# Weaving the latent projections of an attention layer into the last Strassen product of the layer before it

## The chip, the cores and the metric

The kernel runs on one NeuronCore of a Trainium2 chip. The metric is the device time of one execution in microseconds (us). TensorE (PE) multiplies, VectorE (DVE) and ScalarE (ACT) do the elementwise work, GpSimd (POOL) and SyncE (SP) mostly issue DMAs. "Before" took 1385.39 us, the median of three runs (1384.32 to 1385.72).

## The reference

A backbone of two layers over 256 latent tokens and 256 context tokens, model width 1024, all in float32. Layer 0 mixes tokens with a bidirectional chunkwise mLSTM, layer 1 with multi-head latent attention; behind each mixer stands a gated convolutional FFN of inner width 2816, and behind every sub-layer a gated residual with LayerNorm. The place of this change is the seam between the FFN of layer 0 and the attention of layer 1:

```python
x  = layer_norm(ALPHA * x + gate * ffn(h))            # end of layer 0, both streams
h  = x * (1 + scale) + shift                          # input of the attention
def _mla_kv(h, w_dkv, kv_norm, w_ukv, ang):
    ckv, k_rope = split(h @ w_dkv, [256])             # 256 + 64 columns
    if ang is not None: k_rope = axial_rope(k_rope, *ang)
    kv = rms_norm(ckv, kv_norm) @ w_ukv               # 8 heads x (128 key + 128 value)
def _mla_q(h, w_dq, q_norm, w_uq, ang):
    q = rms_norm(h @ w_dq, q_norm) @ w_uq             # 384 columns; 8 heads x (128 + 64)
y = attend(q_latent, [k_context; k_latent], [v_context; v_latent]) @ w_out
```

The latent stream alone is put out, so in layer 1 the context gives keys and values only, and no queries. Its norm, its projection `dkv` and what follows are still needed before the first scores.

## The kernel before, in words

**Products in three matmuls.** Every float32 operand is held as a high and a low part in the type fp32r. `mm3` (lines 398 to 401) issues three matmuls for each product: high by high, high by low, low by high. The halves come from `split` (line 403): ACT casts the high part (line 404), DVE subtracts it to get the low one (line 405).

**Weights as a stream.** `Stream` holds all weight chunks (128 x 1024 floats, 512 KB) in one written-out order, made by `_plan`. SP's queue loads a chunk into a raw buffer (line 293); `_split` casts it on ACT (line 335) and subtracts on DVE (line 338) into a `w` tile (three of them) or, for chunks called wide, into two tiles of the class `u`. There are 31 `u` tiles for nearly everything that is large, and 15 half-size ones (`s2`). `use` hands the next chunk to a product and splits up to eight chunks ahead, as far as tiles and a limit (`st.limit`) allow; `pump` moves the limit and splits up to it.

**Who orders the work.** The program text gives each instruction its priority; a scheduler orders each engine's queue at compile time with an estimate of the times, and each engine then runs its queue in that order. Inside `manual_schedule` for PE, PE's own order is the program's. Background work (`bg`) is written as generators, of which `tick` runs the next steps, `drain` all of them; that too only sets the place in the program.

**The last product of layer 0** (`w_fout0`, line 1368 on) multiplies the FFN's activations by its output weights, both halves of the tokens and of the columns, in Strassen-like products. The first four products (yt2, y11, yt3, yt1) run chunk by chunk in turn, six chunks each, 24 steps. Then come y21, yt4 and y22 in the order `YLAST`: y21 chunks 0 and 1, yt4 0 to 5, y21 2 to 5, y22 0 to 5. A chunk is twelve matmuls of 512 columns (line 1403), the last one six. The activations of these three products were written to DRAM before and are read again by `operand`: one read of up to 256 KB on ACT's queue (line 1384), a copy on ACT (line 1390) and a subtraction on DVE (line 1391) three calls later. There are 18 such reads; in the first four products `operand` is called at every second step from step 11 on, seven times, then once a chunk.

**The seam.** The residual add (`add`, lines 1461 and 1462) and the norm by sums (`z_norm`: squares on ACT, line 1511, roots, line 1515, scaling on ACT, line 1518) make `z`, two row tiles for the latent tokens and two for the context. `ln_T` transposes `z` on PE (line 1214, four transposes into one PSUM tile), applies scale and shift (lines 1221 to 1223) and splits into `hl` (latent) or `hc` (context) (lines 1226, 1227). In the old order the generator `latent` gets its first tick behind y21 chunk 2, does the norm of both tiles in one step and puts its four groups of transposes behind y22 chunks 0, 1, 2 and 3. All of y22 is done before `mla_down` begins:

- `dkv` of the latent tokens (48 matmuls of 320 columns), then the whole `context` generator (residual add and norm of the context tiles), then the latent rows (`dkv_rows`: RMS norm by lines 1525 to 1528, rotary key, copies, line 1563);
- `dq` (48 matmuls of 384 columns), `pump`, the transposes `ckT` of the latent rows (line 1575), the RMS norm of the queries `cq`;
- `ctx_T`, the 16 transposes of the context's `z`; `ukn(1)`, the latent keys (48 matmuls of 256 columns); `uv((2, 3))`, the latent values; `dkv` of the context with its rows.

`mla` goes on with the transposes `cqT` (line 1672), the rotary queries `qr` (18 matmuls), `ckT` of the context, rope on `qr` (lines 1536 to 1538, 1699, 1700), `queries(0)` and `(1)`, `ukn(0)`, `uv((0, 1))`, `rotary(0)` and the loop over heads. The residual for the attention's output (`ln_x`, lines 1242 and 1243, with loads and writes on POOL's queue) runs from `bg` in between. PE's written order covers `YLAST` and `mla_down`, not the first four products and not `mla`.

**The end of attention.** The output product `aout` is followed by `ln_rows` (lines 1156 to 1188), `ln_T` and the first chunks of the second FFN (`fin1`). Between the steps of that norm `st.pump(fi + QB)` and `st.pump(fi + QC)` allow fin1's chunks 2 and 3, then 4 and 5, to be split.

Of the kernel before, what the change touches and what calls it, by code (L numbers as in the profile page):

```python
# [57 lines left out]
         [("y21", j) for j in range(YTURN, 6)] + [("y22", j) for j in range(6)])  # L58
# [13 lines left out]
def _plan():  # L72
# [35 lines left out]
    for n, j in YLAST:  # L108
        add((n, 0, j), cols[j])
    for c, m in enumerate((3, 3, 2)):  # L110
        add(("dkv", 0, c), m * 320, True)
    for c in range(4):
        add(("dq", 0, c), 768, True)
    for c in range(2):
        add(("ukn", 0, c), 1024, True)
    for c in range(2):
        add(("uv", 0, c), 1024, True)
    for c, n in enumerate((2, 1)):
        add(("uqr", 0, c), n * 512)
    for c in range(3):  # L120
        add(("uqn", 0, c), 1024)
# [249 lines left out]
class K:  # L371
# [774 lines left out]
    def ln_rows(self, pss, xres, gate, fin=None):  # L1146
# [3 lines left out]
        for t in range(2):  # L1150
# [33 lines left out]
            if fine and t == 0:  # L1184
                nc.scalar.activation(z[:, 0:512], z[:, 0:512], AF.Identity, bias=nm, scale=rs)
            else:
                nc.vector.tensor_scalar(z[:, 0:512], z[:, 0:512], mv[:, 0:1], rs, op0=ALU.subtract, op1=ALU.mult)
            nc.scalar.activation(z[:, 512:1024], z[:, 512:1024], AF.Identity, bias=nm, scale=rs)
# [179 lines left out]
    def w_fout0(self, x1d, kv0, lat_T, down):  # L1368
# [5 lines left out]
        parts = [(names[n], i) for n, i in YLAST]  # L1374
# [41 lines left out]
        for i in range(6):  # L1416
            for name, ps, x in (("yt2", p6, "S2"), ("y11", p1, "1"), ("yt3", p7, "S3"), ("yt1", p5, "S1")):
# [7 lines left out]
                if n >= 11 and n % 2:  # L1425
                    operand()
# [39 lines left out]
        def latent():  # L1466
            yield from add(1, lo, p7)
            for _ in self.z_norm(z[2:4], sums[2:4]):
                pass
            yield  # L1470
            yield
# [6 lines left out]
        with self.tc.manual_schedule(engines={mybir.EngineType.PE}):  # L1478
            for name, i in YLAST:
                if (name, i) == ("y21", YTURN):  # L1480
                    self.drain()
                    self.bg = [latent()]
                w = st.use((name, 0, i))
                ps, more = {"y21": (p1, True), "yt4": (p7, True), "y22": (p5, True)}[name]
                prod(ps, names[name], w, i, more)
                if name == "yt4" and i in (0, 3):
                    rows(1 if i == 0 else 0)
                if (name, i) == ("yt4", 3):
                    for b in range(2):
                        nc.vector.tensor_tensor(p5[b], p5[b], t[b], op=ALU.subtract)  # L1490
                    self.bg = [add(1, hi, v)]
                if name == "y22" and i < 2:
                    next(low)
                self.tick(2 if name == "y22" and i else 1)
                operand()
                if (name, i) == ("y21", 5):
                    low = add(0, lo, p1)
            self.drain()
            self.fa = self.fd = None
            down(context(), z)  # L1500


    def z_norm(self, zs, sums):

        nc = self.nc
        for z, v in zip(zs, sums):
# [6 lines left out]
            yield  # L1513
# [3 lines left out]
            nc.vector.tensor_tensor(v[:, 0:1], v[:, 0:1], v[:, 2:3], op=ALU.mult)  # L1517
            nc.scalar.activation(z, z, AF.Identity, bias=v[:, 0:1], scale=v[:, 2:3])
            yield
# [95 lines left out]
    def mla_down(self, hl, hc, context, ctx_T):  # L1615

        nc, st = self.nc, self.st
        kv0 = [x[0] for x in st.order].index(("ukn", 0, 0))
        wd = [st.use(("dkv", 0, c), hold=True) for c in range(3)]
# [3 lines left out]
        nc.vector.memset(self.krT[64:128, 1].bitcast(F32), 0.0)  # L1623
        rows = self.dkv_mm(hl, wd)
        for _ in context:
            pass
# [356 lines left out]
```

## Time and profile before

| what | value |
|---|---|
| median of three runs | 1385.39 us |
| profiled execution | 1388.08 us, of which 1386.3 us are its span |
| granted TensorE clock, mean | 0.993 |
| PE busy | 1356.3 us (98%) |
| DVE, ACT, POOL busy | 1061.5, 705.3, 122.5 us |
| DMA moved | 291.86 MB |
| y22's first transposes to the first scores | 1034.4 to 1118.3 us |

A row of a timeline has the start, the length, the engine with its line, the operation, output and inputs, and in brackets the idle time of the engine ahead of it with what ended it. When several like instructions follow each other they make one row (x12). Matmuls overlap, so one matmul's length is longer than the distance to the next. In the list of waits stand the engine and line that waited, the one that ended the wait, the total in us, the number of waits and the longest.

### The profile page before, as it was taken

Reading aid. Unit: us, or ns where it says so; the run is one execution under the profiler, and the core shown is the slowest. Engines: PE = TensorE matmul, PEld = TensorE weight load, DVE = VectorE, ACT = ScalarE, POOL = GpSimd, SP = SyncE. Lnnn points to the kernel's source line nnn. Section 1 sums busy time; section 2 is a strip of 40 time slices with the busy share of each in tenths; the row PEclk is TensorE's granted clock in tenths of the full one; section 3 lists DMA queues with packets and bytes.
Section 4 is the critical chain, followed back from the end, with each engine's and each line's share of the span. In section 5 each row is a group of like instructions: output and inputs, shape, how many; then the busy total and the mean of one; then the engine's idle time right before and its main releaser. Section 6 shows DMA issues by size and latency. Waiting matters only on the chain.

```text
span 1386.3 us, 19100 instructions
## 1 busy us (share of the span) xinstructions
PE 1356.3 (98%) x6903; PEld 1143.7 (83%) x6903; DVE 1061.5 (77%) x1710; ACT 705.3 (51%) x1189; POOL 122.5 (9%) x215
## 2 busy tenths in 40 slices
PE   7999999999999999999999999999998999999997
PEld 3788888888788888878798888888877988999986
DVE  6599757687698697788799878668788689777773
ACT  6585534435444545374643434334578467455560
POOL 0033000011011011120002000001100100000000
PEclk9999999999999999999999999999999999999999
DMA  9689847789656364756747877735867226357750
GB/s 336 223 290 324 290 154 248 238 280 308 216 196 209 100 234 137 245 193 223 239 142 246 298 229 236 237 113 163 248 249 242 85 84 221 107 189 227 208 183 31
DMA packets 94014, 291.86 MB, mean 211 GB/s; under 512 B 11704, under 2 KB 20536, under 8 KB 93920
## 3 DMA queue, kind: packets, MB, share of 16 engines
q1 hardware_dynamic: 67808, 215.64, 47.0%
q0 software_dynamic: 17472, 57.57, 13.4%
q10 hardware_dynamic: 8640, 17.44, 3.5%
q8 instruction: 54, 0.88, 0.3%
q14 instruction: 40, 0.33, 0.1%
HBM read 260.02 MB, written 30.58 MB: 210 GB/s over the span
## 4 chain that ended last, share of the span: by engine, by line
PE 91%; ACT 3%; DVE 3%; DMA 2%; issue 1%; SPq 0%; DVEq 0%; ACTq 0%
PE fin L399 9%; PE fin L400 9%; PE fin L401 9%; PE y L1403 7%; PE tok L399 6%; PE tok L401 6%; PE tok L400 6%; PE qk L399 4%; PE qk L401 4%; PE qk L400 4%; PE y L400 3%; PE y L401 3%; PE y L399 3%; PE up L399 2%; PE up L400 2%; PE up L401 2%
## 5 line engine op out<-in xcount | busy, mean ns | idle before, releaser
L338 DVE TENSOR_TENSOR w<-raw,w 128x1024 fp32r<-128x1024 f32 x286 | 344.1, 1206 | 165.0 <-ACT w L335 164.2
L335 ACT CAST w<-raw 128x1024 fp32r<-128x1024 f32 x286 | 297.0, 1039 | 326.7 <-PE fin L401 100.8
L400 PE MATMUL fin<-h,w 128*128 128x256 f32 (+1 forms) x696 | 231.7, 333 | 0.0
L401 PE MATMUL fin<-h,w 128*128 128x256 f32 (+1 forms) x696 | 231.4, 333 | 0.0
L399 PE MATMUL fin<-h,w 128*128 128x256 f32 (+1 forms) x696 | 231.2, 333 | 0.1
L528 DVE SCALAR_TENSOR_TENSOR junk<-ar,bc 128x1024 f32<-128x1024 f32 x128 | 155.8, 1217 | 4.8 <-ACT bc L570 2.9
L401 PEld LDWEIGHTS fin<-h,w 128*128 128x128 f32 x696 | 132.2, 190 | 12.9
L399 PEld LDWEIGHTS fin<-h,w 128*128 128x128 f32 x696 | 131.9, 190 | 13.2 <-ACT h L1226 0.3
L400 PEld LDWEIGHTS fin<-h,w 128*128 128x128 f32 x696 | 132.2, 190 | 12.8 <-DVE h L1227 0.2
L399 PE MATMUL qk<-xc,w 128*128 128x512 f32 x256 | 100.7, 393 | 0.0
L401 PE MATMUL qk<-xc,w 128*128 128x512 f32 x256 | 99.9, 390 | 0.0
L400 PE MATMUL qk<-xc,w 128*128 128x512 f32 x256 | 99.8, 390 | 0.0
L399 PEld LDWEIGHTS qk<-xc,w 128*128 128x128 f32 x256 | 48.1, 188 | 10.1 <-issue 0.4
L401 PEld LDWEIGHTS qk<-xc,w 128*128 128x128 f32 x256 | 48.1, 188 | 10.0
L400 PEld LDWEIGHTS qk<-xc,w 128*128 128x128 f32 x256 | 48.1, 188 | 9.6
L399 PE MATMUL up<-hT,w 128*128 128x512 f32 x128 | 50.4, 394 | 0.5 <-ACT hT L404 0.5
L338 DVE TENSOR_TENSOR wu<-raw,wu 128x1024 fp32r<-128x1024 f32 (+3 forms) x37 | 43.0, 1177 | 10.2 <-ACT wu L335 10.0
L400 PE MATMUL up<-hT,w 128*128 128x512 f32 x128 | 50.1, 392 | 0.5 <-DVE hT L405 0.5
L401 PE MATMUL up<-hT,w 128*128 128x512 f32 x128 | 50.1, 391 | 0.3 <-DVE w L405 0.3
L399 PE MATMUL tok<-w,hT 128*128 128x512 f32 x128 | 49.8, 389 | 0.0
L400 PE MATMUL tok<-w,hT 128*128 128x512 f32 x128 | 49.8, 389 | 0.0
L401 PE MATMUL tok<-w,hT 128*128 128x512 f32 x128 | 49.8, 389 | 0.0
(436 smaller groups left out, 2970.5 us busy)
## 6 DMA issues: line engine op xcount, KB each, us to landing
raw<-in_ws SPq DMA_DIRECT2D x287, 512.0 KB, 4.5
ar<-in_adaT SPq DMA_DIRECT2D x80, 512.0 KB, 4.8
adaw<-in_ada_w SPq DMA_DIRECT2D x32, 256.0 KB, 6.7
raw<-in_ws POOLq DMA_DIRECT2D x13, 512.0 KB, 7.1
xmd<-xr POOLq DMA_DIRECT2D x16, 256.0 KB, 5.2
xcd<-cv POOLq DMA_DIRECT2D x16, 256.0 KB, 4.9
xs<-xmd POOLq DMA_DIRECT2D x16, 256.0 KB, 5.5
od<-o ACTq DMA_DIRECT2D x16, 256.0 KB, 2.4
```

Of the source, the lines that this page charges most:

```text
L335: k.nc.scalar.copy(h[:, :cols], src)
L338: k.nc.vector.tensor_sub(l[:, :cols], src, h[:, :cols])
L399: mm(out, w[0], x[0], start=start, stop=False)
L400: mm(out, w[0], x[1], start=False, stop=False)
L401: mm(out, w[1], x[0], start=False, stop=stop)
L528: nc.vector.scalar_tensor_tensor(o, w, 1.0, self.bc[j], op0=ALU.mult, op1=ALU.mult, accum_out=col[:, k, j:j + 1])
L1403: nc.tensor.matmul(ps[b], a[:, p, ts], w[q][:, cs], start=j == 0 and n == 0 and not more, stop=j == 10 and n == 2, skip_group_check=True)
```

## The change

`YLAST` takes in three more entries (dkv and dq, and the transposes ckT, between chunks of y22):

```diff
-         [("y21", j) for j in range(YTURN, 6)] + [("y22", j) for j in range(6)])
+         [("y21", j) for j in range(YTURN, 6)] + [("y22", j) for j in range(4)] +
+         [("dkv", 0), ("y22", 4), ("dq", 0), ("ckT", 0), ("y22", 5)])
```

The weight order follows it (dkv's three chunks before y22 chunk 4, dq's four before y22 chunk 5) and goes on with ukn, uqr, two chunks of uqn, uv, the last of uqn; it was ukn, uv, uqr, uqn. `mla_down` is gone: its parts are `lat_kv` (weights of dkv, latent dkv and its rows) and `lat_q` (dq and the RMS norm of its rows), called from the loop over `YLAST`, and the rest moved into `mla`. PE's written order now covers the first four products, `YLAST` and `mla` up to `rotary(0)`.

```diff
-                if n >= 11 and n % 2:
+                if n >= 5 and n % 4 != 3:
                     operand()
...
         def latent():
             yield from add(1, lo, p7)
-            for _ in self.z_norm(z[2:4], sums[2:4]):
-                pass
-            yield
-            yield
+            yield from self.z_norm(z[2:4], sums[2:4])
+            for _ in range(3):
+                yield
             yield from lat_T(z[2:4])
...
+            if name == "dkv":
+                self.drain()
+                self.lat_kv(hl)
+                continue
+            if name == "dq":
+                self.lat_q(hl)
+                st.pump(kv0 + 2)
+                continue
+            if name == "ckT":
+                self.dkv_T(self.rows, 2)
+                continue
             if (name, i) == ("y21", YTURN):
                 self.drain()
                 self.bg = [latent()]
+                self.tick(3)
...
-                self.tick(2 if name == "y22" and i else 1)
+            self.tick(4 if name == "y22" and i else 1)
```

So the latent transposes come in two groups of eight, behind y22 chunks 1 and 2. `z_norm` does its three phases (squares, roots, scaling) for both row tiles together, with a yield after each phase; it had two yields for each tile. `context` has the same body and is now stepped through inside `mla`:

```diff
+    def mla(self, hc, context, ctx_T, residual):
+        for _ in range(2):
+            next(context)
         st.limit = [x[0] for x in st.order].index(("aout", 0, 0))
+        self.wk = [st.use(("ukn", 0, c)) for c in range(2)]
...
+        next(context)
+        self.ukn(1)
+        for _ in context:
+            pass
...
         queries(0)
+        ctx_T()
         queries(1)
+        rows = self.dkv_mm(hc, self.wd)
+        st.unhold("dkv")
+        rows = self.dkv_rows(rows, 0)
+        self.wv = [st.use(("uv", 0, c)) for c in range(2)]
+        self.uv((2,))
+        qr = []
...
+        self.dkv_T(rows, 0)
+        self.uv((3,))
         self.ukn(0)
         self.uv((0, 1))
+        for _ in residual:
+            pass
         rotary(0)
```

Behind the attention the splits of fin1's chunks 2 to 5 are queued behind the last two scalings of the norm, on DVE and ACT, and stand in the program behind its transposes:

```diff
-        k.tick(1)
-        st.pump(fi + QB)
-        k.tick(1)
-        st.pump(fi + QC)
+        k.tick(2)
         k.drain()
+        with tc.issue_after(k.lv.ins), tc.issue_after(k.la.ins):
+            st.pump(fi + QC)
```

`k.lv` and `k.la` are the last DVE and ACT scalings of `ln_rows`; `issue_after` fixes only the order of issue on an engine.

159 lines of the change are left out of this document (74 added, 85 removed).

## Prediction

> **What bounds the kernel now.** I read the page first, for the engine that sets the time.
>
> ```profile
> PE 1356.3 (98%) x6903; PEld 1143.7 (83%) x6903; DVE 1061.5 (77%) x1710; ACT 705.3 (51%) x1189; POOL 122.5 (9%) x215
> ...
> PE 91%; ACT 3%; DVE 3%; DMA 2%; issue 1%; SPq 0%; DVEq 0%; ACTq 0%
> ```
>
> TensorE (PE) is busy in 98% of the span and holds 91% of the chain that ended last. The change removes no matmul, so it can only win time in which PE stood still or ran slowly. The list of what PE waited for, cut to 980 to 1200 us where the touched code runs, says how much that is:
>
> ```profile
> PE ckT L1575 <- DVE ckr L1528: 4.8, 2, 3.0
> PE zT L1214 <- ACT z L1518: 1.9, 1, 1.9
> PE zT L1214 <- DVE z L1187: 1.8, 1, 1.8
> PE qr L399 <- ACT cqT L1674: 0.6, 1, 0.6
> ```
>
> The reader sees three waits that the change moves (ckT, the first zT, qr) and one that stands behind the attention and whose work keeps its place (zT on z L1187). The timeline of PE shows what follows a wait:
>
> ```profile
> 1036.65 0.55 PE L1214 MATMUL zT<-ident,z 128*128 128x128 f32 x3 [1.94 <-ACT z L1518]
> 1036.95 4.58 PE L1403 MATMUL y<-w,fz 128*128 128x512 f32 x12
> 1041.38 0.60 PE L1214 MATMUL zT<-ident,z 128*128 128x128 f32 x4
> 1041.73 3.00 PE L1403 MATMUL y<-w,fz 128*128 128x512 f32 x12
> ...
> 1070.85 0.33 PE L1575 MATMUL ckT<-ident,ckr 128*128 128x128 f32 x1 [2.97 <-DVE ckr L1528]
> 1073.06 1.33 PE L1575 MATMUL ckT<-ident,ckr 128*128 128x128 f32 x5 [1.88 <-DVE ckr L1528]
> 1074.18 3.62 PE L1214 MATMUL zT<-ident,z 128*128 128x128 f32 x16
> 1077.45 0.56 PE L399 MATMUL kn<-ckT,wu 128*128 128x256 f32 x1
> ```
>
> ```profile
> 1034.40:1052.40 18.00, 16.06 (x72) 13.02 (x72) 15.98 (x27) 16.95 (x31) 0.00 (x0) 0.91 0.45 145
> 1067.90:1078.00 10.10, 5.27 (x24) 5.05 (x25) 8.27 (x24) 8.48 (x22) 2.16 (x4) 0.67 0.73 242
> ```
>
> After the 1.94 us wait the same twelve matmuls take 4.58 us and then 3.00 us, and the stage table (us, busy PE, PEld, DVE, ACT, POOL, granted clock, DMA share, GB/s) grants 0.91 of the clock over those 18 us: 0.09 x 18 = 1.6 us lost. In the second stage the 16 zT start from 1074.18 to 1077.45, 0.204 us apart, where eight transposes at full clock take 0.87 us, 0.109 each (row below); that is 1.5 us lost, and the five ckT lose (1074.18 - 1073.06) - 5 x 0.109 = 0.6 us, the first kn some 0.3 us.
>
> ```profile
> 1128.01 0.87 PE PT L1764 x8
> ```
>
> So what can be won at most is 1.94 + 1.6 (first zT), 2.97 + 1.88 + 2.4 (ckT and the zT behind it) and 0.6 (qr): **11.4 us**, 0.8% of the time.
>
> [...]
>
> **The change part by part.**
>
> *The latent norm and its transposes.* Three background steps run before the product y21[2], the norm of both row tiles goes in three joint phases, and the transposes come in two bursts of eight behind y22[1] and y22[2], instead of four bursts of four from y22[0] on. One product of twelve matmuls of 512 columns stands in front more. In the stage of the first four products (row below) 179 such matmuls take 40 us, 0.223 each:
>
> ```profile
> 960.00:1000.00 40.00, 40.00 (x179) 33.11 (x178) 27.84 (x29) 16.82 (x20) 6.61 (x10) 1.00 0.76 203
> ```
>
> That is 2.7 us; z came 1.94 us late, so this alone covers it. Besides, the adds that feed the norm waited behind weight splits on DVE (VectorE):
>
> ```profile
> 1021.59 0.69 DVE L1461 TENSOR_TENSOR zp<-y,gate 128x512 f32<-128x512 f32 x1
> 1022.20 1.22 DVE L338 TENSOR_TENSOR w<-raw,w 128x1024 fp32r<-128x1024 f32 x1
> ...
> 1026.62 0.68 DVE L1461 TENSOR_TENSOR zp<-y,gate 128x512 f32<-128x512 f32 x1
> ```
>
> The second add started 5 us after the first, both traced one product apart; traced together they should follow each other. The wait goes: -3.5 us. What is late next is the copying of hl: eight pairs on ACT (ScalarE) between the first burst and dkv. ACT was busy 16.95 of 18.00 us there.
>
> ```profile
> 1047.79 0.60 PE L1214 MATMUL zT<-ident,z 128*128 128x128 f32 x4
> ```
>
> ```profile
> 1050.42 0.83 ACT L335 CAST wu<-raw 128x768 fp32r<-128x768 f32 x1
> ```
>
> The dkv product now starts two products (y22[4], y22[5], 18 matmuls, 4.0 us) earlier, but the last burst ends some 6.5 us earlier too (behind y22[2] and 16 transposes, 1034.4 + 2 x 2.7 + 1.7 = 1041.5, for the 1048.4 of the row), and four of the reread activations are copied before. I take 0.2 us of waiting, from 0 to 1.0 (hl[7] caught behind casts of dq's weights, 0.83 us each as in the second row).
>
> *dkv and dq between the chunks.* In the old order the context norm stands ahead of the latent rows on ACT and DVE: PE leaves dkv at 1059.40 (first row below), and the second tile's row comes with the wait that ends at 1073.06 (above). Now y22[4] (2.7 us) and dq lie behind dkv:
>
> ```profile
> 1059.40 0.34 PE L399 MATMUL dq<-wu,hl 128*128 128x384 f32 x1
> ...
> 1067.55 0.34 PE L401 MATMUL dq<-wu,hl 128*128 128x384 f32 x1
> ```
>
> 48 matmuls in 8.3 us. The cover is 11 us. The chain it has to hide can be read off the context's own pass, which had little ahead of it (PE's last dkv, then ACT, then DVE):
>
> ```profile
> 1095.92 0.31 PE L401 MATMUL dkv<-wu,hc 128*128 128x320 f32 x1
> ```
>
> ```profile
> 1095.82 0.38 ACT L1525 ACTIVATE ckr<-dkv 128x256 f32<-128x256 f32 x1 [2.44 <-PE dkv L401]
> ...
> 1096.63 0.47 ACT L1526 ACTIVATE rs<-rs,keps 128x1 f32<-128x1 f32 x2
> ```
>
> ```profile
> 1098.31 0.48 DVE L1528 TENSOR_SCALAR ckr<-dkv,rs 128x256 f32<-128x256 f32 x1
> ...
> 1099.22 0.18 DVE L1563 COPY ckr<-ckr 128x64 f32<-128x64 f32 x1
> ```
>
> ```profile
> L1675 DVE SCALAR_TENSOR_TENSOR cqT<-cqT,sm 128x256 fp32r<-128x256 f32 x3 | 1.4, 472 | 0.0
> ```
>
> PE is past its last dkv at 1096.1 (48 matmuls in 7 us, 0.15 each), the last copy ends at 1099.4: 3.3 us, 1.4 of them the three cqT operations of the group row, which ran between. 11 us hide that with room, so the ckT waits go: -7.2 us. Without that cover it would be 1 to 2 us.
>
> *The new wait: cqT.* The queries' rows are now wanted right behind dq, with six ckT transposes (0.7 us) and y22[5] (six matmuls, 1.3 us) as cover, 2.0 us. The same chain on 384 columns, without the cqT operations, is 3.3 - 1.4 plus about 0.5 for the wider square and scaling: 2.4 us. Behind the waiting cqT stands all of PE. So at least 0.4 us; with a ckT copy and a weight split (1.2 us) caught in between up to 2.0, and 1.6 us of lost clock on top if it passes the length of the wait at the first zT. The wait of 0.6 us at qr cost no clock, 1.00 being granted in its stage, the second row:
>
> ```profile
> 1078.00:1097.00 19.00, 18.88 (x126) 17.68 (x124) 8.87 (x19) 8.11 (x21) 0.00 (x0) 1.00 0.06 19
> 1097.00:1118.00 21.00, 20.48 (x133) 18.63 (x134) 20.20 (x40) 11.38 (x21) 2.17 (x4) 1.00 0.45 151
> ```
>
> I take +1.5.
>
> *qr* now follows ukn(1), 48 matmuls, so its wait of 0.6 goes. *Context norm behind the latent keys:* its squares and scalings (rows below: on ACT four of the first kind, 0.9 with their read-out, and two of the second; on DVE four adds of 0.7) fall beside ukn(1), qr and queries(0), 84 matmuls at 0.15 (126 in 18.88 us, above), some 12 us of PE:
>
> ```profile
> 1029.38 0.71 ACT L1511 ACTIVATE jk<-z,zs 128x512 f32<-128x512 f32 x1
> ...
> 1035.36 1.24 ACT L1518 ACTIVATE z<-z,zs 128x1024 f32<-128x1024 f32 x1
> ```
>
> The chain is 4 x 0.9 + 2 x 1.2 + 4 x 0.7, some 9 us. Hidden: 0 us, and up to 3 if ACT's queue holds much else. The residual's loads and writes move on POOL's queue with it; no wait of PE in the list names POOL.
>
> *Context keys:* dkv_rows(0) is covered by uv((2,)), 12 matmuls of 512 columns, 2.7 us, against a chain of 1.9 to 3.3 us, with rope rows as possible neighbours on DVE. Bounds 0 and 1.1, I take +0.5.
>
> *DVE in front of the scores.* DVE is the fullest engine beside PE. In the attention itself:
>
> ```profile
> 1118.00:1160.00 42.00, 41.49 (x271) 37.02 (x270) 36.79 (x76) 28.64 (x63) 5.00 (x9) 1.00 0.27 96
> ```
>
> Between 1067.9 and 1118 DVE did 8.27 + 8.87 + 20.20 = 37 us (rows above); with the context's four adds and the small steps of its norm, done ahead of that so far and now behind the last product, some 41, while PE's part of that stage, without its waits and slow stretches and with y22[5] in it, is 50 - 2.97 - 1.88 - 0.6 - 2.4 + 1.3 = 43 us. Of the 41, the residual and the last v (7 us) need not precede the scores. DVE was full for 20.20 of 21.00 us before without a wait of PE. Bounds 0 and 3, I take +0.7.
>
> *Rereads in the first four products.* 14 instead of 7 of the 18 reads are issued there, from ACT's queue, with a copy on ACT and a subtraction on DVE of 512 columns each, half of a split (1.2 us for 1024 columns, above): 7 x 0.6 = 4 us more on engines that have room (27.84 of 40 us on DVE, 16.82 on ACT in the stage's row), and 4 us less where ACT was full. 0 us, and up to 1. The weights' order on SP's queue changes only within the stage; ukn is wanted at about 1066, 11 us earlier than now, and its second half was split by 1061.7:
>
> ```profile
> 1060.50 1.21 DVE L338 TENSOR_TENSOR wu<-raw,wu 128x1024 fp32r<-128x1024 f32 x1
> ```
>
> *The end of attention.* Four weight chunks of fin1 are now split behind the last norm instead of ahead of it. In the old trace the last of them starts at 1179.43, PE's last y at 1184.42:
>
> ```profile
> 1179.43 1.21 DVE L338 TENSOR_TENSOR wu<-raw,wu 128x1024 fp32r<-128x1024 f32 x1
> ```
>
> ```profile
> 1184.42 0.28 PE L401 MATMUL y<-wu,oT 128*128 128x256 f32 x1
> ```
>
> So the wait there (z L1187, above) hangs on PE itself: nothing to win. Behind the norm, four splits of 1.2 us on DVE, and about as much on ACT, lie beside the copies of h. Bounds -0.3 and +2.5, I take +0.5.
>
> **Sum:** -3.5 - 7.2 - 0.6 + 0.2 + 1.5 + 0.5 + 0.7 + 0.5 = -7.9 us. The profiled execution took 1388.08 us with a span of 1386.3; the median of the runs is 1385.39, 2.7 lower. Off the median: 1377.5 us. By the bounds alone the forecast lies between 1374 (new waits nearly nil) and 1385 (all of them at their ends).
>
> **The rivals.** *The waits move.* Two new waits (cqT and the scores, say) each pass the length that costs clock: 2 x (1.9 + 1.6) = 7.0 us back instead of 3.4. For it: the cover of cqT is shorter than its chain. Against: no other cover is. Gain some 4 us: 1382.
>
> *The chains stay as late.* ACT and DVE are ordered when the kernel is compiled, by an estimate; if splits still go ahead of the adds and rows, the waits stay though the program is rewritten. For it: the add held up by 5 us. Against: each chain has gained a cover longer than its lateness. 1385.4.
>
> [...]
>
> *Slower: a queue held by a tile slot.* In the old trace ACT stood still for 6.63 us in front of a copy of v, because its target tile (one of 31) came free only with dkv; DVE stood behind it:
>
> ```profile
> 1090.98 2.40 ACT L404 CAST v<-v 128x512 fp32r<-128x512 f32 x4 [6.63 <-PE dkv L401]
> ```
>
> It cost PE nothing, since PE had all of dkv to do. I count 30 to 34 such tiles wanted at ctx_T in the new order (kn 8, wd 6, wk 4, wv 4, z, ckT, krT, qn, hc 4). If ACT is held there again, hc comes late with only queries(1), 2.1 us, as cover, and DVE's 41 us wait behind it: at the rate of the attention stage (36.79 of 42.00, 0.88) they need 47, and with 6.6 us of standing still PE comes out of its 43 us some 10 late. With one lost stretch of clock (1.6) and the waits of the sum at cqT and fin1 (2.0) that is 14 us against the 11.4 won: 1387 to 1389. It decides from the point where the hold outlasts queries(1). [...] Against it: dkv's own first matmuls free hc and wd tiles.
>
> **How the numbers follow.** Forecast 0.60, waits move 0.18, slow clock 0.03, chains as late 0.06, slower 0.13. A measurement of this kernel tells about 0.2% (2.8 us) from no change. Faster: 0.60 + 0.18 + 0.03, less a tail of the second, 0.80; within: the unchanged case with that tail, 0.07; slower: 0.13. The range runs from 1373.5 (all 11.4 us, rounded out) to 1386.5, which leaves out the slower rival.
>
> **What would show it.** No wait of PE at zT behind y22[1]; ckT behind y22[4]/dq without wait; a granted clock of 1.00 from 1030 to 1060; a wait of 0.4 to 2 us at cqT; dkv of the context without a wait. I am wrong if hc or ckT of the context is waited for by more than 3 us, if the first fin1 matmuls stand behind splits, or if a wait appears in the first four products.

## The result: no difference that can be measured

The changed kernel takes 1385.86 us (median of 12 executions, 1384.04 to 1388.58), the kernel before, measured again beside it, 1386.46 us (12 executions): ratio 0.9995, 95% interval 0.9986 to 1.0004. The forecast of 1377.5 us was 8.4 us too low: 7.3 us because a gain of 7.9 us was forecast and 0.6 us came, and 1.1 us because the kernel before, measured again, was slower than the 1385.39 us from which the forecast started. Two executions of the kernel before in later rounds, of 1688.40 and 2751.32 us, are left out of the ratios. The profiled execution of the changed kernel took 1384.17 us, with a span of 1382.1 us.

### The profile page after: what moved, and what is told of

Read it like the earlier page. It is cut to its first block, busy times and chain, and to the rows that moved or that the text cites. A ratio compares the mean times of both kernels' runs of the same rounds, so it can differ in the third digit from the quotient of the medians.

```text
span 1382.1 us, 19113 instructions
## 1 busy us (share of the span) xinstructions
PE 1353.0 (98%) x6903; PEld 1139.1 (82%) x6903; DVE 1062.1 (77%) x1710; ACT 704.6 (51%) x1189; POOL 122.5 (9%) x215
## 4 chain that ended last, share of the span: by engine, by line
PE 90%; DVE 4%; ACT 3%; DMA 2%; issue 1%; SPq 0%; DVEq 0%; ACTq 0%
PE fin L404 9%; PE fin L405 9%; PE fin L406 9%; PE y L1409 7%; PE tok L404 6%; PE tok L406 6%; PE tok L405 6%; PE qk L404 4%; PE qk L406 4%; PE qk L405 4%; PE y L405 3%; PE y L406 3%; PE y L404 3%; PE up L404 2%; PE up L406 2%; PE up L405 2%
```

## The profile after

TensorE is the bound as before (page of the changed kernel, first part; before it was busy 1356.3 us):

```profile
PE 1353.0 (98%) x6903; PEld 1139.1 (82%) x6903; DVE 1062.1 (77%) x1710; ACT 704.6 (51%) x1189; POOL 122.5 (9%) x215
```

The list of PE's waits in the changed kernel, 980 to 1200 us, answers to the four rows shown of before (total, times, longest; the lines of the changed file are up to 20 higher):

```profile
PE zT L1220 <- DVE z L1192: 2.5, 1, 2.5
PE dkv L404 <- DVE qn L1721: 1.2, 1, 1.2
PE fin L404 <- ACT h L1232: 1.1, 1, 1.1
PE o L404 <- ACT PT L409: 1.0, 1, 1.0
PE y L1409 <- ACT w L340: 0.9, 1, 0.9
PE y L1409 <- DVE w L343: 0.7, 2, 0.5
PE cqT L1682 <- DVE cq L1547: 0.5, 1, 0.5
PE ckT L1594 <- DVE ckr L1547: 0.4, 1, 0.4
PE zT L1220 <- ACT z L1537: 0.3, 1, 0.3
PE fin L405 <- DVE h L1233: 0.3, 1, 0.3
PE ckT L1594 <- DVE ckr L1582: 0.3, 1, 0.3
PE kn L405 <- DVE ckT L1599: 0.2, 1, 0.2
```

The waits aimed at are gone: the first zT, qr, and of 4.8 us at ckT 0.7 are left. In their place stand nine smaller ones, and the wait behind the attention has grown. The gaps of at least 0.15 us between PE's matmuls from 1000 us on add up to 9.9 us before and 9.4 us after. **Nearly all of the idle time has only moved.**

Where it moved shows in the three stretches from the first row of y on `fs` to the first scores, on to the first `fin1`, and on to the first row of fout1 (us; busy PE, PEld, DVE, ACT, POOL; granted clock, DMA share, GB/s). First the kernel before, then the changed one:

```profile
941.72:1118.31 176.59, 169.17 (x859) 146.20 (x858) 142.44 (x238) 106.40 (x181) 13.14 (x21) 0.97 0.62 199
1118.31:1190.08 71.77, 69.14 (x427) 61.08 (x426) 61.60 (x116) 46.55 (x88) 5.53 (x10) 0.98 0.42 147
1190.08:1317.17 127.09, 127.09 (x1059) 127.09 (x1057) 91.08 (x143) 68.96 (x113) 7.56 (x14) 1.00 0.60 187
```

```profile
941.11:1112.63 171.52, 166.86 (x859) 142.64 (x858) 142.80 (x239) 105.97 (x181) 12.60 (x20) 1.00 0.65 207
1112.63:1185.02 72.39, 67.82 (x428) 59.90 (x426) 56.64 (x109) 42.83 (x84) 6.10 (x11) 1.00 0.32 107
1185.02:1312.98 127.96, 127.55 (x1056) 126.97 (x1057) 95.80 (x148) 72.64 (x117) 7.56 (x14) 1.00 0.67 206
```

Up to the scores this pair shows 5.1 us won, 2.8 of them idle time and 2.3 less busy time, at a granted clock of 1.00 for 0.97; behind the scores 0.6 and 0.9 us are given back. But the clock differs from one execution to the next, from 0.995 to 0.999 in those of the changed kernel. Over the timed executions its mean is 0.9968 for the changed kernel and 0.9945 to 0.9948 for the one before (in the rounds of the experiments below); the two profiled executions lie on the far sides of these means, at 0.999 and 0.993. They make the change look 3.9 us faster; the typical executions differ by 0.6.

**Two places where waits came up.** In the last product (ACT's timeline of the changed kernel):

```profile
1026.68 0.72 ACT L1527 ACTIVATE jk<-z,zs 128x512 f32<-128x512 f32 x1 [1.28 <-DVE zs L1524]
...
1029.63 1.28 ACT L1532 ACT_TABLE_LOAD   x1
1030.93 0.48 ACT L1532 ACTIVATE zs<-zs,keps 128x1 f32<-128x1 f32 x2
1031.32 1.98 ACT L340 CAST w<-raw 128x1024 fp32r<-128x1024 f32 x2
1033.20 1.24 ACT L1537 ACTIVATE z<-z,zs 128x1024 f32<-128x1024 f32 x1
```

and PE's timeline beside it:

```profile
1032.40 0.73 PE L1409 MATMUL y<-w,fz 128*128 128x512 f32 x2 [0.86 <-ACT w L340]
1033.66 5.31 PE L1409 MATMUL y<-w,fz 128*128 128x512 f32 x22 [0.53 <-DVE w L343]
```

The weight casts of y22's first two chunks (the row at 1031.32) stand on ACT behind four squares, a table load and two roots. Before, the first chunk was cast ahead of the squares, at 1027.71, and only the second one, at 1034.42, stood behind them (ACT's timeline of before):

```profile
1027.71 1.05 ACT L335 CAST w<-raw 128x1024 fp32r<-128x1024 f32 x1 [1.58 <-PE y L1403]
...
1030.91 1.28 ACT L1515 ACT_TABLE_LOAD   x1
...
1033.11 1.23 ACT L1518 ACTIVATE z<-z,zs 128x1024 f32<-128x1024 f32 x1
...
1034.42 1.03 ACT L335 CAST w<-raw 128x1024 fp32r<-128x1024 f32 x1
```

Then, PE waited at zT for z, and the late cast of the second chunk was hidden by that wait. Now the norm is one product earlier and zT one product later, so the squares go ahead of the first chunk's cast, and PE comes to that cast before it comes to zT.

Behind the attention (ACT, then DVE, then PE of the changed kernel):

```profile
1182.73 1.03 ACT L340 CAST w<-raw 128x1024 fp32r<-128x1024 f32 x1
1183.66 1.01 ACT L1227 ACTIVATE zm<-zT,lnB,lnA 128x256 f32<-128x256 f32 x2
```

```profile
1183.79 1.22 DVE L343 TENSOR_TENSOR w<-raw,w 128x1024 fp32r<-128x1024 f32 x1 [1.42 <-ACT w L340]
1184.93 0.54 DVE L1229 TENSOR_SCALAR zm<-zT,lnA,lnB 128x256 f32<-128x256 f32 x1
```

```profile
1182.42 1.53 PE L1220 MATMUL zT<-ident,z 128*128 128x128 f32 x12 [2.51 <-DVE z L1192]
1185.02 0.50 PE L404 MATMUL fin<-h,wu 128*128 128x256 f32 x2 [1.06 <-ACT h L1232]
```

The split issued right behind the last scalings runs ahead of the first copies of h, for which PE waits 1.06 us, and the transposes wait 2.51 us where they waited 0.27 and 1.84. This place the prediction had named, with a smaller price.

## Experiments

Each ran in five rounds beside the kernel before; the ratio given, with its 95% interval, is to that kernel. I began with three theories: **G**, the idle time is given back elsewhere, and the two profiles are a lucky pair; **C**, the slow clock belongs to the waits and is paid again in each execution; **T**, the old place of fin1's splits has a cost of its own. b_ marks a kernel made from before, x_ one made from the changed kernel.

### Noise and the end of attention

**base_again**: before, unchanged. 

> The kernel before, unchanged, to see how its executions scatter in span and granted clock. Theory G (given back, and a lucky pair of profiles): the 4 us of slow clock in the one profile of before are at its bad end; the executions scatter between about 0.993 and 0.998, the spans between 1382 and 1387 us, with a median span near 1384.5. Theory C (the clock loss belongs to the waits and comes each time): all executions near 0.993 and spans near 1386.

1387.08 us, ratio 1.0002 (0.9993 to 1.0011). The profiled execution shows the three stretches at half clock that the first one showed, at 1036.8, 1070.9 and 1187.0 us, and a mean clock of 0.993 as there. So they were no accident, against G. But the eleven executions scatter from 0.993 to 0.996 in clock and from 1383.8 to 1386.7 us in span, where C expected all near 0.993 and 1386: most executions lose clock, not all the same amount.

**x_pump**: the changed kernel with fin1's splits at their old place.

```diff
-        k.tick(2)
+        k.tick(1)
+        st.pump(fi + QB)
+        k.tick(1)
+        st.pump(fi + QC)
         k.drain()
-        with tc.issue_after(k.lv.ins), tc.issue_after(k.la.ins):
-            st.pump(fi + QC)
```

> The changed kernel with the splits of fin1's chunks 2 to 5 put back between the steps of the norm, as before; all else as changed. Theory G: the tail of the change gives back 1 to 2 us (the split ahead of the copies of h), so this is faster than the changed kernel by 1 to 2 us, ratio to before about 0.998. Rival T: the old place now has its own cost (a split falls into the chain of the last norm), then this equals the changed kernel, 0.9995.

1386.76 us, 0.9999 (0.9990 to 1.0009). PE's list of waits:

```profile
PE zT L1220 <- DVE z L1192: 4.5, 1, 4.5
```

T's 0.9995 lies inside the interval, G's 0.998 does not. The wait is 2.0 us longer than in the changed kernel, since two splits fall into the norm's own chain on DVE; the time is 0.9 us longer by the medians, which the intervals do not tell apart. T is right for this order of the engines, though in the kernel before the old place is the better one (next run).

**b_tail**: before with the change's new end of attention alone (the same edit the other way round). 

> The kernel before with only the splits of fin1's chunks 2 to 5 moved behind the last scalings of the norm. Theory G: slower than before by 1 to 2.5 us (ratio 1.001 to 1.002), since a cast of 1.0 us on ACT and a subtraction of 1.2 us on DVE come ahead of the copies of h. Theory C: no difference.

1387.66 us, 1.0009 (1.0001 to 1.0018): slower by about 1.2 us by the ratio, a little under the 1.001 that G expected at the least, and just clear of no difference. The wait behind the attention is 2.5 us as in the changed kernel, and the stretch from fin1 to fout1 takes 127.96 us as there. This part of the change is a small loss by itself.

**x_best**: the changed kernel with chunks 2 and 3 split ahead of the norm, and 4 and 5 behind the copies of h.

```diff
+        st.pump(fi + QB)
         k.tick(2)
...
-                nc.scalar.copy(hi, tmp[:, c])
-                nc.vector.tensor_sub(lo, tmp[:, c], hi)
+                self.la = nc.scalar.copy(hi, tmp[:, c])
+                self.lv = nc.vector.tensor_sub(lo, tmp[:, c], hi)
```

> The changed kernel with chunks 2 and 3 of fin1 split ahead of the norm and chunks 4 and 5 behind the last copies of h, so that no split lies between the norm and the first fin1 matmul. Theory G: the wait ahead of the first fin1 matmul shrinks by 1 to 1.5 us against the changed kernel; ratio to before about 0.9975 to 0.9985. Theory C: equal to the changed kernel.

1383.53 us, **0.9972 (0.9964 to 0.9981)**, 2.3 us below the changed kernel by the medians. Its last two stretches:

```profile
1113.75:1185.46 71.71, 68.27 (x427) 59.88 (x425) 58.04 (x111) 43.91 (x85) 6.13 (x11) 1.00 0.36 122
1185.46:1312.42 126.96, 126.96 (x1056) 126.87 (x1057) 94.02 (x146) 71.84 (x116) 7.56 (x14) 1.00 0.67 199
```

71.71 and 126.96 us for 72.39 and 127.96: 1.7 us of the 2.3 are seen in these rows. G, which put the loss there, is right; C expected no change.

### The price of the slow clock

**b_fill**: before, with matmuls whose result nobody reads (fillers) run in PE's waits, so that the waits stay and PE is busy.

```diff
+            if kp == 0 and self.warm is not None:
+                self.fill(self.st.last, 8)
...
+    def fill(self, w, n):
+        idle = self.ps("idle")
+        for _ in range(n):
+            self.nc.tensor.matmul(idle, w[:, 0:128], w[:, 0:512], start=True, stop=True)
...
+        if t0:
+            self.fill(self.wd0, 12)
...
+                if t0 and t and not k:
+                    self.fill(self.wd0, 8)
...
```

> The kernel before with TensorE kept busy in its own waits: 8 matmuls of 512 columns into a PSUM tile that nobody reads ahead of the first latent transposes (wait 1.94 us in the trace of before), 12 ahead of the first ckT transposes (2.97 us) and 8 ahead of the second group (1.88 us). The outputs do not change; the fillers are added work, about 0.2 us each by the 128x512 matmuls of the trace, so 1.6, 2.5 and 1.6 us, less than the wait that each stands in. It tells what the slow clock costs when the waits stay. Theory C (each of these waits brings one or two stretches of 3.4 us at half clock, and these are paid in nearly every execution): the two stretches near 1037 and 1071 us, 10.2 us of half clock, are gone, the mean clock is 0.997 in place of 0.9945, and the time is 2.0 to 4.0 us shorter although every wait is still there: ratio 0.997 to 0.9985. Theory G (the stretches of the profiled execution were chance, the typical execution doesn't pay them): within 0.5 us of before, ratio 0.9997 to 1.0005.

1383.39 us, **0.9975 (0.9964 to 0.9985)**, mean clock 0.9976. The work that PE waits for comes no earlier, and 3.4 us are gone, as C expected: about as much as any version of the change ever won. Adding 28 useless matmuls beats moving the projections.

**b_fillall**: the same with 11 fillers behind the attention. 

> The kernel before with fillers in all of its long waits: those of b_fill (8 ahead of the first latent transposes, 12 and 8 at the ckT transposes) and 11 between the last matmul of attention's output projection and the first transposes of the layer norm behind it (waits of 0.27 and 1.84 us). The outputs do not change; the fillers are added work. Theory C (a wait of about 2 us costs its length and a stretch of 3.4 us at half clock): the last stretch, near 1183 us, goes too, no half clock is left in the profiled execution, the mean clock is 0.999, and the time is 0.8 to 1.7 us shorter than that of b_fill: ratio 0.9963 to 0.9970. If that stretch costs nothing, since the few matmuls in it are short: 0.9975, as b_fill.

1383.48 us, 0.9980 (0.9971 to 0.9989), clock 0.9985; no half clock before the end in its profile. No gain over b_fill by the times: the expected 0.8 to 1.7 us did not come, though the mean clock rose from 0.9976 to 0.9985. In the profiles the two stretches behind the scores take 1.0 us less than in b_fill (71.22 and 126.81 us for 71.80 and 127.20). But the first row of y on `fs` starts at 941.86 us in this profile and at 940.52 in b_fill's, a difference of 1.3 us in work that neither run touches; a gain of 1 us cannot be told from such times.

**b_fillck**: fillers at ckT alone. 

> The kernel before with the fillers at the ckT transposes alone (12 and 8); the wait of 1.94 us before the first latent transposes stays bare. The outputs do not change. Theory C: the stretch of 6.8 us near 1071 goes, which my prediction priced at 2.4 us of slow clock, and the one of 3.4 us near 1037 (1.6 us) stays: 2.4 us shorter than before, ratio 0.9980 to 0.9986. If the first wait brings its stretch only now and then: 0.9975 to 0.9980, near b_fill.

1384.21 us, 0.9988 (0.9979 to 0.9997), clock 0.9974: 2.0 us by the medians, a little under the 2.4 that C expects; its 0.9980 to 0.9986 lie inside the interval.

**b_half**: b_fillall with 3, 8, 5 and 4 fillers, so that part of each wait is back. 

> b_fillall with the fillers cut from 8, 12, 8 and 11 to 3, 8, 5 and 4, so that the waits of before come back in part (about 1.0 to 1.4 us at the first latent transposes, 0.8 and 0.5 us at ckT, 0.9 to 1.3 us at the layer norm behind attention). The outputs do not change. If the clock is halved for a cell of 3.413 us only when TensorE worked less than half of the cell before: none of these waits reaches 1.7 us in a cell, the profiled execution has no half clock, the mean clock is that of b_fillall (0.9985), and the time is within 0.5 us of it: 1383.0 to 1384.0 us, ratio 0.9975 to 0.9983, although about 3.5 us of bare waiting is back. If the slow clock has a price for each us of wait: a third of the loss comes back, 1384.3 us or more, clock 0.997.

1382.99 us, 0.9979 (0.9970 to 0.9987), clock 0.9983, no half clock in the profile, though 6.3 us of gaps stand in it where b_fillall has 2.0. So the slow clock was not paid per us of waiting: 4.3 us more of gaps, and a mean clock of 0.9983 for 0.9985. Which wait brings it shows in cells of 3.41 us, the length of the single stretches at half clock in before (1037.12 to 1040.53 and 1187.31 to 1190.72 us). Their edges are counted from the trace's first full clock (in before 13.12 us, and 1024.0 us later, 300 cells, the first stretch at half clock begins); a cell at half clock is called slow. The cell with the wait and the one behind it, in before at the first zT:

```profile
1033.71:1037.12 3.41, 1.47 (x9) 0.91 (x8) 1.96 (x4) 3.41 (x6) 0.00 (x0) 1.00 0.14 38
1037.12:1040.53 3.41, 3.41 (x10) 2.64 (x9) 3.38 (x7) 3.41 (x6) 0.00 (x0) 0.50 0.26 98
```

in b_tail, with the same wait of 1.9 us lying otherwise across its cells:

```profile
1034.79:1038.20 3.41, 1.72 (x9) 1.50 (x10) 2.85 (x5) 3.41 (x5) 0.00 (x0) 1.00 0.29 74
1038.20:1041.61 3.41, 3.41 (x18) 2.83 (x18) 3.41 (x6) 3.41 (x8) 0.00 (x0) 1.00 0.32 75
```

and in b_half, at the wait behind the attention:

```profile
1181.69:1185.10 3.41, 1.89 (x17) 1.64 (x15) 1.71 (x7) 1.82 (x4) 0.00 (x0) 1.00 0.00 0
1185.10:1188.52 3.42, 3.00 (x26) 2.77 (x24) 3.42 (x10) 3.42 (x11) 0.00 (x0) 1.00 0.00 0
```

PE worked 1.47 us of the first cell, and the next is granted half the clock; 1.72 and 1.89 us, and the clock stays whole. The same wait of 1.9 us cost a slow cell in before and nothing in b_tail, with the cells' edges at 1033.71 us in the one and at 1034.79 in the other.

**x_fill**: the changed kernel with 6 fillers ahead of y22's first chunk and 11 behind the attention. 

> The changed kernel, with 6 fillers ahead of the product that waits for its weight cast near 1031.5 us (0.86 and 0.53 us) and 11 ahead of the transposes of the layer norm behind attention (2.51 us); the outputs do not change. It compares the two kernels with the slow clock taken out of both. Theory G (the change only moves the idle time: 9.9 us before, 9.4 us after, both from 1000 us on): the time is that of b_fillall within 0.7 us, ratio 0.9960 to 0.9972. My prediction's reason (the change takes 5.8 us of idle time away): 3 us or more below b_fillall, 0.9945 or lower. If the changed kernel hardly loses clock, as its one profiled execution says: 0.9985 to 0.9995, as it was.

1384.37 us, 0.9985 (0.9976 to 0.9994), clock 0.9982: 0.9 us above b_fillall by the medians. The absolute ratio that G expected (0.9960 to 0.9972) is missed, because b_fillall had gained less than expected; the comparison with b_fillall, which the run was for, speaks against 3 us of the change's own. The ratio also touches the third expectation, a kernel that hardly loses clock, but the mean clock rose from 0.9968 to 0.9982, so it does lose some.

**x_fillend**: with 9 fillers behind the attention alone. 

> The changed kernel with 9 fillers ahead of the transposes of the layer norm behind attention alone (a wait of 2.51 us in its trace). The outputs do not change. By the cell rule this wait brings a half-clock cell in about 3 executions of 4, and the other waits of the changed kernel (at most 1.39 us close together) bring none: the mean clock rises from 0.9968 to 0.998, and the time falls by 0.5 to 1.2 us from that of the changed kernel, ratio 0.9985 to 0.9992, as x_fill. If the wait near 1031.5 us has its share: 0.9992 to 0.9997.

1384.56 us, 0.9985 (0.9976 to 0.9994), clock 0.9985. So the changed kernel too loses clock, behind its longest wait: the mean clock rises by 0.0017. By the ratios that is about 1.4 us (0.9995 to 0.9985), though these intervals overlap. The wait at y22, 1.39 us, costs no clock that x_fill shows (0.9982 with fillers there too). And with the clock held in both, the changed kernel is not measurably ahead: 0.9985 against 0.9979 and 0.9980 of b_half and b_fillall. G holds in this form.

### The last product

**b_norm**: before with the earlier, joint latent norm and the new reread cadence alone (the diff of `latent`, `z_norm` and the ticks in the section on the change). 

> The kernel before with the change's earlier latent norm alone: both tiles' squares together, both roots together, three free steps and four transposes' steps per product, and the reread cadence that goes with it; the projections, the context norm and attention stay where they were. Theory G (the squares, the table load and the roots stand on ScalarE ahead of the next weight casts whichever way the norm is cut, so TensorE waits for the norm or for the cast behind it): the wait of 1.94 us before the first latent transposes is gone, and waits of 1.0 to 2.2 us for a weight cast and its DVE subtraction stand just ahead of it, near 1031 us; the time is within 1 us of before, ratio 0.9993 to 1.0007. My prediction's reason (the earlier norm removes 1.94 us of idle and 1.6 us of slow clock and puts nothing in place): 3.5 us shorter, ratio 0.9975.

1385.64 us, 0.9991 (0.9980 to 1.0001). PE's waits in it:

```profile
PE y L1403 <- DVE w L338: 1.1, 2, 0.9
...
PE y L1403 <- ACT w L335: 0.5, 1, 0.5
```

The zT wait of 1.94 us is gone and 1.4 us stand in front of it for the weight cast, as G has it; the ratio lies close to 0.9993, the lower end of G's range, and the 0.9975 of my reason lies outside the interval. In this profile the pieces bring no slow cell there: PE works 2.03 us of the cell that holds them.

**x_reread**: the changed kernel with the old cadence of the rereads.

```diff
-                if n >= 5 and n % 4 != 3:
+                if n >= 11 and n % 2:
                     operand()
```

> The changed kernel with the rereads of the activations at their old cadence (from the twelfth product of the first four on, every second one). My prediction's term for the rereads is 0. Theory G gives the same: within 0.6 us of the changed kernel, ratio 0.999 to 1.0003 to before. If the old cadence crowds the last product instead, where ScalarE now has the squares, the two roots, the weight casts and the reread casts together, the wait for the weight cast near 1031 us grows from 1.3 us to 2.5 us or more and the time is 1 to 3 us longer than that of the changed kernel.

1389.77 us, 1.0017 (1.0008 to 1.0026), 3.9 us above the changed kernel. From its list of PE's waits, and ACT's timeline:

```profile
PE y L1409 <- ACT w L340: 4.1, 1, 4.1
```

```profile
1031.39 0.60 ACT L1396 CAST fz<-zr 128x512 fp32r<-128x512 f32 x1
1031.89 1.24 ACT L1537 ACTIVATE z<-z,zs 128x1024 f32<-128x1024 f32 x1
...
1033.04 1.23 ACT L1537 ACTIVATE z<-z,zs 128x1024 f32<-128x1024 f32 x1
1034.17 0.60 ACT L1396 CAST fz<-zr 128x512 fp32r<-128x512 f32 x1
1034.68 1.04 ACT L340 CAST w<-raw 128x1024 fp32r<-128x1024 f32 x1
```

The cast is now behind two reread copies and both scalings as well, as the rival in the expectation has it, and the price is higher than its 1 to 3 us. The earlier norm needs the new cadence; whether the cadence alone would change the kernel before was not run.

**x_top**: x_best with the order on ACT written out: the cast of y22's first chunk ahead of the squares, the next ahead of the roots, and one root on a constant early, for the table load of 1.28 us (at 1029.63 us in the changed kernel; here none stands between 1025 and 1040 us).

```diff
+        pin(nc.scalar.activation(self.tiny(1, "rs"), self.keps, AF.Sqrt, bias=self.keps, scale=1.0))
...
-                self.tick(3)
+                self.tick(2)
+                self.pin = pin
             w = st.use((name, 0, i))
+            if name == "y21" and i in (4, 5):
+                self.tick(1)
...
```

(`pin` keeps casts, squares, roots and scalings in the program's order.) 

> The kernel that issues the output splits behind the end of the last layer norm (x_best) with the weight casts of the last product put in order by hand: one root on a constant early, so that the table load lies in an idle part of ScalarE, the squares behind the weight cast of the product two ahead, the roots behind the next one. Theory G: in the trace of x_best the casts at 1032.4 us stand behind four squares (2.8 us), the table load (1.28 us) and two roots (0.5 us); with the cast ahead of the squares TensorE finds its weights, the waits of 1.47 and 0.53 us near 1033 go, at most 0.7 us come back at the latent transposes, and the time is 0.8 to 1.8 us shorter than that of x_best: ratio 0.9957 to 0.9967 to before. Theory C alone: x_best has almost no half clock left (0.9975), so only the idle time can be saved, 1.3 us. The rival: the norm is then late for the latent transposes, a wait of 1.5 us or more stands there, and the time is that of x_best or worse, 0.997 to 0.998.

1383.36 us, 0.9972 (0.9961 to 0.9984), as x_best. The waits of 1.47 and 0.53 us at y22 are gone, with 0.24 us at the transposes and 0.53 us behind them in their place, and the gaps from 1000 us on fall from 8.8 to 7.2 us, as planned; the median does not follow. The ratio is the one that the rival expected, but not by its mechanism, a wait of 1.5 us or more at the transposes. The profiled execution has a slow cell behind the attention (from 1182.9 us) that x_best's has not, but the mean clock is the same over the timed executions, 0.9976 and 0.9975. Why the 1.6 us of gaps aren't seen in the times stays open; the intervals, 2 to 3 us wide, could hide most of them.

**x_topfill**: x_top with 10 fillers behind the attention. 

> x_top (the changed kernel with the splits behind the end of the norm and the weight casts ahead of the squares) with 10 fillers ahead of the transposes of the layer norm behind attention; the outputs do not change. x_top has 7.2 us of idle time from 1000 us on, 2.7 us less than before, and its profiled execution still lost one stretch of 3.4 us at half clock near 1183 us. If idle time and clock simply add up: 0.8 to 1.5 us shorter than x_top and 1.5 to 2.7 us shorter than b_fillall: ratio 0.9950 to 0.9963. If the stretch of x_top's profile is rare: 0.9970, as x_top.

1382.83 us, 0.9975 (0.9965 to 0.9986), clock 0.9979. By median the lowest of all, but the ratio is not, and its interval covers x_best's 0.9972 and b_fill's 0.9975. The 0.9950 to 0.9963 of simple addition are missed. No version beats another of these three measurably.

## Why the prediction was wrong

**Where it was right.** Most of the ckT waits went (4.85 us became 0.73), the qr wait went, DVE's full queue did not hold up the first scores at 1112.63 us (the last gap of PE ahead of them is 0.21 us, at 1100.8), and ACT was held by PE's dkv in front of a copy of hc for 0.32 us only, for the 6.6 us of the slower rival. The rereads cost 0.2 us for the 0 of the sum: the wait of 0.21 us for a weight at 1004.3 us, which b_norm has too and x_reread has not. cqT waited, as foretold, for 0.53 us in place of 1.5. The range of 1373.5 to 1386.5 us holds the measured time, but that is no merit: it reached beyond no change at all, and the gain that was forecast did not come.

**"The wait goes: -3.5 us" (latent norm).** It went, but I asked only what is late next *behind* the transposes. On ACT a weight cast of y22 stood among the norm's own operations, as late as z itself, and with the norm one product earlier the squares also went ahead of the cast of y22's first chunk. 1.94 us of idle came back as 1.39 (0.86 + 0.53). b_norm shows this alone, and in x_top, where the casts go ahead of the squares and the roots, PE no longer waits at y22's first chunk.

**"The end of attention, +0.5" (bounds -0.3 and +2.5).** The mechanism was named, but the size was far from the 0.5 that I took, though inside the bounds. With the clock at 1.00 in both, b_fillall (below) and the changed kernel (above) stand against each other:

```profile
1115.09:1186.31 71.22, 70.34 (x438) 61.97 (x436) 61.48 (x116) 46.40 (x88) 5.52 (x10) 1.00 0.45 148
1186.31:1313.12 126.81, 126.81 (x1056) 126.81 (x1057) 91.08 (x143) 68.96 (x113) 7.56 (x14) 1.00 0.62 187
```

72.39 - 71.22 + 127.96 - 126.81 = 2.3 us, of which 0.6 is the longer wait at `o` (1.0 for 0.4 us) in the attention itself; 1.7 are left for the end. The fillers do not shift this: b_fillck, which has none there and full clock too, takes 71.22 and 126.82 us. My criterion "the first fin1 matmuls stand behind splits" came true. x_best, which changes only this, gets 2.3 us back.

**"Context keys", a wait of dkv named as none.** dkv of the context waits 1.16 us: ACT has three weight casts between the transposes and the first copies of hc, and DVE their three subtractions. With ckT's 0.73, cqT's 0.53, the context's zT (0.35), kn (0.21) and o (0.6 more), the new waits sum to 3.6 us where I had 2.9.

**The clock, 1.6 + 2.4 us.** I took the slow stretches of one execution as lost each time, and as won in full. One slow cell lowers the mean clock by 0.5 x 3.413 / 1386 = 0.0012. From b_fillall's 0.9985, before loses 3.2 cells in the mean (0.9946), the changed kernel 1.4 (0.9968). b_fillall's 2.8 us make 0.9 us for a cell, b_fill's 3.4 us for 2.4 cells (0.9976 from 0.9946) make 1.4. So the change wins an estimated 1.8 x 0.9 = 1.6 to 1.8 x 1.4 = 2.5 us of clock, not 4.0. The wait behind the attention brings slow cells in both kernels (in before 0.50 granted from 1187.31 to 1190.72 us; in the changed kernel fillers there alone raise the mean clock from 0.9968 to 0.9985); I left it out of the sum. No run shows the slow clock without the waits, to which the chances give 0.03: with fillers in three of the waits the mean clock rose from 0.9946 to 0.9976 (b_fill), and with fillers behind the attention as well the profile has no half clock before the end (b_fillall).

**What no list of gaps shows.** A matmul's row is longer than the distance to the next one (0.31 for 0.15 us at dkv), so a matmul that starts late by less than that leaves no gap. At full clock, from the first row of y on `fs` to the first scores, PE's matmuls and transposes take 165.0 us from start to start in b_half, without the gaps and the fillers, and 166.9 in the changed kernel, without its gaps. The 48 matmuls of the context's dkv take 7.78 us for 7.04, y on `fz` 46.1 for 45.5, kn 11.9 for 11.6. At dkv six of the first steps last 0.20 to 0.38 us for 0.15, while hc is still being copied; at y the first step behind a wait or behind transposes lasts 0.31 to 0.34 us for 0.23. These 1.9 us stand nowhere in my sum: I priced each late operand as one wait ahead of the first matmul, and did not ask how the matmuls behind it go on.

The terms together, 1.4 (norm) + 0.2 (rereads) + 1.2 (1.7 for 0.5 at the end) + 0.7 (3.6 for 2.9 of new waits) + 1.5 to 2.4 (clock) + 1.9 (late without a gap), are 6.9 to 7.8 us; 7.3 lie between the -7.9 of the sum and the -0.6 measured, whose interval reaches from -1.9 to +0.6. No run has the weaving of dkv and dq alone; what it won and cost is read from the traces, not shown by an experiment of its own.

Two sums of the prediction are off. The bound of 1385 us leaves out the "up to 3" of the context norm and the "up to 1" of the rereads; with them its own bounds reach 1389. And by its own numbers "The waits move" wins 4.3 us, which is 1381, not 1382. That rival came nearest in mechanism, but it moved two waits, and nearly all have moved. The nearest number, 1385.4 of "The chains stay as late", is luck: those waits did go.

## What to carry to other kernels

Before you count a wait as won, look at the whole queue of the engine that is late: whatever stands beside the late instruction, and was hidden by the wait, is next, and whatever the moved work now stands ahead of becomes late itself. Measure a stretch from start to start as well, because a list of gaps misses matmuls that are late by less than their own length. A part of a change that is only meant to make room (here the new end of attention) is worth its own run: alone it cost 0.09%, and with it mended the rest gained 0.28%. And compare the granted clock over all timed executions before reading a difference of 0.3% from one pair of profiles.

## What the runs showed of the hardware

**Half clock came in cells of 3.413 us.** In before the clock is full from 13.12 us on for 1024.0 us, 300 cells. The stretches behind that, half and full in turn, take 3.41, 30.72, 6.83, 109.23, 3.41 and 191.14 us, which is 1, 9, 2, 32, 1 and 56 cells; the last stretch, at half clock up to the end of the span, takes 4.44 us and is no whole number. In the changed kernel the clock is full from 13.40 to 1378.73 us, 400 cells. The edges differ between executions: one is at 1033.71 us in before, at 1034.79 in b_tail, at 1034.92 in b_half. Leaving out the end of the program, PE worked 0.38, 1.47 and 1.59 us of the cells ahead of slow ones in before (at 1067.84, 1033.71 and 1183.90 us), and 1.61 us of the slow cell at 1071.25 us, behind which a second one came. With 1.72 us (b_tail) and 1.89 us (b_half) the next was full, and so it was in before with 2.29 us or more, which is all of its other cells up to the end of the program. Two cells are exceptions: one of the changed kernel's, with 1.53 us of work, had no slow cell behind it, and one of x_fill had one after 2.16 us:

```profile
1180.79:1184.20 3.41, 1.53 (x12) 1.29 (x12) 1.50 (x6) 2.49 (x5) 0.00 (x0) 1.00 0.00 0
1184.20:1187.61 3.41, 2.26 (x16) 2.05 (x17) 3.41 (x8) 3.41 (x9) 0.00 (x0) 1.00 0.37 126
```

```profile
1084.23:1087.64 3.41, 2.16 (x11) 1.54 (x11) 3.41 (x9) 3.41 (x9) 0.09 (x1) 1.00 0.87 302
1087.64:1091.05 3.41, 3.41 (x15) 3.41 (x14) 2.51 (x6) 1.85 (x5) 0.98 (x2) 0.50 0.69 241
```

so but for these two it turns between 1.61 and 1.72 us of work in a cell, about half of 3.413; why the two differ was not shown. A wait of 1.94 us was enough for a slow cell behind it (in before, from 1037.12 us). The shortened waits of b_half, with 1.89 to 2.57 us of work in the cells that hold them, brought no slow cell.
